# DeltaNet values turned by VectorE and a transfer instead of by TensorE

## The chip, the cores and the metric

The kernel runs on one core of a Trainium2 chip. The metric is the device time of one execution in microseconds (us), taken as the median of several runs. A profile is one further execution, recorded by the hardware; its span goes from the first to the last instruction.

## What is computed

One layer of a hybrid decoder on x of 1024 tokens by 2048 channels in float32, and a final RMSNorm. An input projection of the normalised x gives the columns of three groups: a gated MLP with mixing along the sequence (4 groups of 128), a gated DeltaNet (8 heads of 128), and cross-attention into 256 memory tokens (4 heads of 128). An output projection adds their gated outputs to x. What matters here is the DeltaNet and its values v:

```python
qkv = causal_conv_silu(jnp.concatenate([d_q, d_k, d_v], axis=-1), conv_w[l])
q, k, v = jnp.split(qkv, 3, axis=-1)
...
g = -jnp.exp(dn_a_log[l]) * jax.nn.softplus(d_a + dn_dt_bias[l])
beta = jax.nn.sigmoid(d_b)
o = gated_delta_rule(q, k, v, g, beta)   # per head, chunk by chunk along the tokens
o = rmsnorm(o, dn_norm_g[l]) * jax.nn.silu(d_z)
```

The causal convolution runs along the tokens, four taps per channel. Inside the delta rule each token's row of v is multiplied by a scalar of that token.

## The kernel before

The tokens are handled in two halves (`hf`) of 512, each of which is four tiles of 128 tokens (`NT = 4`). The projections are the bulk of TensorE's work: `project_stage` and `seven` run seven products over blocks of weights in place of eight (sums and differences of operand blocks are formed first), and each float32 operand is split into a high and a low part (`rhi`, `rlo`, `lh`, `ll`), three matmuls per product. They accumulate in the PSUM tiles `acc` and, in some stages, `dn2` and `dn3`. The weights come as tiles `raw` and `kept`, the left operands as `ll` and `lm`.

The DeltaNet runs beside the projections. A head's queries, keys and values are written by the projection to memory (`p_d`) with the channels on the partitions and the tokens along the row, since that suits the convolution. `front` prepares the queries and keys of a pair of heads for one half; `inverse` and `levels` invert the triangular matrices of the chunks; `back_of` calls `front_late` (loads what `front` stored), `levels`, `values`, and `back`, which makes the four `scan_step`s over token tiles and then `heads_out`. There are four pairs of heads and two halves, so `back_of` runs eight times: pairs 0 and 1 for both halves, each followed by a `front` of pair 2 or 3, and later pairs 2 and 3 for both halves.

`values` runs `conv` (one scaling on ScalarE, three multiply-adds on VectorE, SiLU on ScalarE) into a tile `v` of the ring `tn`. The scan wants the tokens on the partitions. So `to_tokens` has TensorE transpose the four 128x128 tiles of `v` against the identity into a PSUM bank (`scan_banks`), and `by_token` scales them, one ScalarE instruction per tile, into the head's `vs`.

The outputs of the heads take another way back to channels on partitions. `turn` has VectorE transpose a 128x512 tile in blocks of 32x32 and stores it to memory, `turned_in` loads it in four transfers, each of which puts one row of blocks in its place, and `normed` reads the loaded tile in the view `four(..., "b t i")`, which walks over four runs of 32 elements. The same pair of helpers is used for the gate (`gate`) and for the gated MLP (`gated`, `spatial`).

The ring `tn` has four tiles, handed out in turn. `values` takes one per head, `qk` (in `front`) one per head for a broadcast row, `all_sums` three per call, and the ring `sums` of the attention stage contains them too. One of the four is taken out of the ring for good ahead of the last four `back_of`:

```python
el = over([abh[:, 0:HT], ring["tn"].bufs.pop()])
```

No instruction goes straight to an engine. Every call is recorded in a `Plan` with its dependencies, and `Plan.issue` lays them all out: `lay` simulates the five engines and the DMA engines with costs per instruction, `late` computes due times from the end, and of nine such layouts the one that the simulation gives the earliest end is issued. Each engine then works through its list in order. All loads and stores named here are issued by SyncE's queue (`Q`). Line 398 of the profile is the line on which all recorded instructions are issued, so groups are told apart by the names of their tiles.

Of the kernel before, what the change touches and what calls it, by code (L numbers as in the profile page):

```python
# [11 lines left out]
AF = mybir.ActivationFunctionType  # L12
# [5 lines left out]
P = 128  # L18
# [4 lines left out]
HT = 512  # L23
# [3 lines left out]
NG, NH, NX = 4, 8, 4  # L27
# [374 lines left out]
def kernel(  # L402
# [29 lines left out]
    V, S, G, PE, Q = R.dve, R.act, R.pool, R.pe, R.sp  # L432
    rank, behind = R.rank, R.behind

    def C(shape, name, dt=F32):
        return sb.tile(list(shape), dt, name=name, tag=name)[:]

    def DT(shape, name, dt=F32):
        return dr.tile(list(shape), dt, name=name, tag=name)[:]
# [41 lines left out]
    def tok(ap):  # L481

        return ap.rearrange("p (t c) -> p t c", c=P)
# [15 lines left out]
    ring = {t: Slots(t, 2, [P, HT]) for t in ("kT", "qT", "vs", "kd", "ai")}  # L499
# [6 lines left out]
    jk = C([P, HT], "jk", mybir.dt.bfloat16)  # L506
# [4 lines left out]
    turn = {"acc": 0, "tp": 0, "dn": 0}  # L511
# [224 lines left out]
    for mt in range(2):  # L736
        t = [ring["ai"](F32R) for _ in range(2)]
# [9 lines left out]
    for h in range(NX):  # L747
        t = ring["vs"](F32R).rearrange("p (s m) -> p s m", s=2)
# [60 lines left out]
    def over(bufs):  # L809
        r = Ring("", 0, None)  # L810
        r.bufs = bufs
        return r
# [38 lines left out]
    r3, ww = ([steps[:, i * P : (i + 1) * P] for i in two] for two in ((0, 1), (2, 3)))  # L851
    scs = [C([P, 12, NT, NH], f"sc{hf}") for hf in range(2)]
    gcs, ecs = ([DT([NT, NH, P], f"{n}{hf}") for hf in range(2)] for n in ("gcd", "ecd"))
    e_d = [[DT([P, NT, P], f"ed{hf}_{h}") for h in range(NH)] for hf in range(2)]
    scan_banks, work = dnr.bufs[0:2], over(dnr.bufs[0:2])
    dnab = over(scan_banks)
# [68 lines left out]
    def to_tokens(*pairs):  # L925
        with R.together():
            for src, tp in pairs:
                for tt in range(NT):
                    PE.transpose(tp[:, tt * P : (tt + 1) * P], src[:, tt * P : (tt + 1) * P], ident)
        return [tok(tp) for src, tp in pairs]  # L930

    def four(t, order):

        return t.rearrange(f"p ({order}) -> p t b i", b=4, t=NT)

    def turn(tile, src, dst):

        V.transpose(four(tile, "b t i"), four(src, "t b i"))
        Q.dma_start(dst, tile)

    def turned_in(o, src):

        v = src.rearrange("(a j) (b n) -> b j a n", a=4, b=4)
        for b in range(4):
            Q.dma_start(o[b * 32 : (b + 1) * 32].rearrange("j (a n) -> j a n", a=4), v[b])

    def conv(which, h, hf, o):
        ct = which * NH + h
        xr = ring["xr"]()
        w = [cw[:, k * 24 + ct : k * 24 + ct + 1] for k in range(4)]  # L950
        if hf == 0:
            G.memset(xr[:, 0:3], 0.0)
            Q.dma_start(xr[:, 3:], p_d[which][h][:, 0:HT])
        else:
            Q.dma_start(xr, p_d[which][h][:, HT - 3 :])
        S.activation(o, xr[:, 3:], AF.Copy, scale=w[3])
        for k in range(3):
            V.scalar_tensor_tensor(o, xr[:, k : k + HT], w[k], o, op0=ALU.mult, op1=ALU.add)
        S.activation(o, o, AF.Silu)

    def by_token(o, src, scale):
        for tt in range(NT):
            S.activation(o[:, tt], src[:, tt], AF.Copy, scale=scale[:, tt : tt + 1])

    def sumsq(o, src):
        for tt in range(NT):
            S.activation(jk[:, 0:P], src[:, tt], AF.Square, accum_out=o[:, tt : tt + 1])

    def qk(h, hf, tiles, hs, gt, bank):

# [2 lines left out]
        beta, edk = (scs[hf][:, i] for i in (0, 4))  # L973
        (kt,) = to_tokens((k, bank))
        sumsq(hs[:, 1], kt)
        V.tensor_scalar(hs[:, 1], hs[:, 1], EPS, None, op0=ALU.add)
        V.reciprocal(hs[:, 3], hs[:, 1])
        V.scalar_tensor_tensor(hs[:, 2], hs[:, 3], -1.0, beta[:, :, h], op0=ALU.mult, op1=ALU.mult)
        V.tensor_tensor(out=hs[:, 3], in0=hs[:, 2], in1=edk[:, :, h], op=ALU.mult)
        by_token(kd, kt, hs[:, 3])  # L980
        e = tok(ring["E"]())
        Q.dma_start(e, e_d[hf][h])
        Q.dma_start(vs, ecs[hf][:, h].partition_broadcast(P))
        by_token(e, e, hs[:, 2])
        (qt,) = to_tokens((q, bank))
        sumsq(hs[:, 0], qt)
        V.tensor_scalar(hs[:, 0], hs[:, 0], P * EPS, P * EPS * EPS, op0=ALU.mult, op1=ALU.add)
        rsqrt_to(hs[:, 4], hs[:, 1])
# [170 lines left out]
    def heads_out(hf, hp, hss, rest):  # L1159
        obs = [vs for kd, ai, vs in rest]  # L1160

        for hs, ob in zip(hss, obs):
            sumsq(hs[:, 5], ob)
            V.scalar_tensor_tensor(hs[:, 6], hs[:, 5], 1.0 / P, hs[:, 0], op0=ALU.mult, op1=ALU.add)
            rsqrt_to(hs[:, 7], hs[:, 6])
            by_token(ob, ob, hs[:, 7])
        for h, (kd, ai, vs) in zip(hp, rest):
            kd, ai, y = (t.rearrange("p t c -> p (t c)") for t in (kd, ai, vs))
            turn(kd, y, o_d[hf][h])
            if h >= NJ:  # L1170
                e = sums()
                Q.dma_start(e, g_d[hf][h - NJ])
                turned_in(ai, o_d[hf][h])
                normed(kd, ai)
                V.tensor_tensor(out=y, in0=kd, in1=e, op=ALU.mult)
                head_done(h, hf, y)
# [36 lines left out]

    def values(hf, hp, gt, qs, ks, hss, rest, inv):
        for i, h in enumerate(hp):
            v = ring["tn"]()
            conv(2, h, hf, v)
            bank = scan_banks[i]
            by_token(rest[i][2], to_tokens((v, bank))[0], hss[i][:, 4])

    def back(hf, hp, gt, qs, ks, hss, rest, inv, ut=None):
        ut = ut or levels(gt, *inv)
# [339 lines left out]
    scan_banks, work = [dnr.bufs[0]] * 2, over(dnr.bufs[0:1])  # L1562
    gdrs = []

    def back_of(p, hf, inv):
        state = front_late(p, hf, inv)
        ut = levels(state[2], *state[-1])
        values(*state)
        back(*state, ut)
# [106 lines left out]
    scan_banks, work = dnr.bufs[0:2], over(dnr.bufs[2:3])  # L1676
# [46 lines left out]
    for n, (tag, to) in enumerate((("gt", mkT), ("inv", mv))):  # L1723
        for i in range(NX // 2):
            t = ring[tag](F32R).rearrange("p (h s m) -> p h s m", h=2, s=2)
# [107 lines left out]
    tn = ring["tn"].bufs  # L1833
# [88 lines left out]
```

## Time and profile before

| | |
|---|---|
| median of 3 runs | 1594.69 us (1593.5 to 1596.71) |
| profiled execution: its own time | 1593.81 us |
| profiled execution: span | 1592.1 us |
| mean granted TensorE clock | 0.997 |
| busy: TensorE, its weight loads | 1570.2 us, 1315.3 us |
| busy: VectorE, ScalarE, GpSimd | 1228.7 us, 963.3 us, 106.7 us |
| moved by the DMA engines | 434.12 MB, 273 GB/s on average |

The busy time of TensorE contains the modelled ends of pipelined matmuls: a 128x512 matmul lasts 0.39 us in the records, but the next one starts 0.23 us after it. The span is shorter than the profiled execution's own time by what lies around the first and last instruction. A row of a group of instructions has the engine, the operation, what it writes and reads, its count, the busy time and the mean time of one in ns, and then the idle time of its engine ahead of it with what ended that. A row of a tile has count, shortest, median and longest duration in ns, and the starts of the first and last in us. A row of a stretch has its length and for each engine the busy time and the number of instructions, then the granted clock, the busy share of the DMA engines and GB/s. A row of the timeline has the start and the length in us.

### The profile page before, as it was taken

Reading aid. Unit: us, or ns where it says so; the run is one execution under the profiler, and the core shown is the slowest. Engines: PE = TensorE matmul, PEld = TensorE weight load, DVE = VectorE, ACT = ScalarE, POOL = GpSimd, SP = SyncE. Lnnn points to the kernel's source line nnn. Section 1 sums busy time; section 2 is a strip of 40 time slices with the busy share of each in tenths; the row PEclk is TensorE's granted clock in tenths of the full one; section 3 lists DMA queues with packets and bytes.
Section 4 is the critical chain, followed back from the end, with each engine's and each line's share of the span. In section 5 each row is a group of like instructions: output and inputs, shape, how many; then the busy total and the mean of one; then the engine's idle time right before and its main releaser. Section 6 shows DMA issues by size and latency. Waiting matters only on the chain.

```text
span 1592.1 us, 24568 instructions
## 1 busy us (share of the span) xinstructions
PE 1570.2 (99%) x8349; PEld 1315.3 (83%) x8349; DVE 1228.7 (77%) x1818; ACT 963.3 (61%) x2006; POOL 106.7 (7%) x143
## 2 busy tenths in 40 slices
PE   8999999999999999999999989999999999999997
PEld 7988888888887888888888878888888888888886
DVE  6977655877589997777789996867658888688875
ACT  6833255535698436787886557765658864344455
POOL 0100010001000100111111001000000000000001
PEclk9999999999999999999999999999999999999999
DMA  9999966888679898786888988999877989778647
GB/s 320 327 317 346 284 171 183 294 292 245 218 246 315 298 325 254 257 250 205 282 281 277 303 244 245 341 325 309 268 245 253 298 298 347 235 263 293 232 146 276
DMA packets 335951, 434.12 MB, mean 273 GB/s; under 512 B 70089, under 2 KB 160466, under 8 KB 335826
## 3 DMA queue, kind: packets, MB, share of 16 engines
q1 hardware_dynamic: 334098, 429.39, 83.3%
q0 software_dynamic: 1088, 2.10, 0.4%
q8 instruction: 66, 1.08, 0.3%
q10 hardware_dynamic: 640, 1.07, 0.2%
q14 instruction: 59, 0.48, 0.1%
HBM read 332.78 MB, written 99.16 MB: 271 GB/s over the span
## 4 chain that ended last, share of the span: by engine, by line
PE 92%; ACT 3%; DMA 2%; DVE 1%; issue 1%; SPq 0%; POOL 0%; POOLq 0%; ACTq 0%; DVEq 0%
PE acc L398 56%; PE dn L398 35%; ACT jk L398 1%; ACT rhi L398 1%; DMA h0d<-tn 1%; SPq L398 0%; DMA tn<-vd 0%; DMA ut<-in_x_dram 0%; DMA kept<-in_mem_dram 0%; DVE rlo L398 0%; DMA raw<-in_w_in_dram 0%; DVE vs L398 0%; ACT vs L398 0%; DVE tn L398 0%; ACT inv L398 0%
## 5 line engine op out<-in xcount | busy, mean ns | idle before, releaser
L398 PE MATMUL acc<-lh,rhi 128*128 128x512 f32 x1024 | 396.2, 396 | 2.9 <-DVE obs L398 1.2
L398 PE MATMUL acc<-lh,rlo 128*128 128x512 f32 x1024 | 382.9, 397 | 0.0
L398 ACT CAST rhi<-raw 128x1024 fp32r<-128x1024 f32 (+1 forms) x148 | 186.6, 1261 | 248.8 <-PE dn L398 133.8
L398 DVE TENSOR_TENSOR rlo<-raw,rhi 128x1024 fp32r<-128x1024 f32 (+1 forms) x148 | 219.3, 1482 | 109.0 <-ACT rhi L398 98.8
L398 PE MATMUL acc<-ll,rhi 128*128 128x512 f32 x688 | 268.0, 395 | 0.8 <-DVE ll L398 0.8
L398 PEld LDWEIGHTS acc<-lh,rhi 128*128 128x128 f32 x1024 | 192.3, 188 | 41.1 <-issue 1.5
L398 PEld LDWEIGHTS acc<-lh,rlo 128*128 128x128 f32 x1024 | 191.9, 188 | 37.4
L398 DVE TENSOR_TENSOR ll<-ll,lh 128x1024 fp32r<-128x1024 f32 x122 | 148.5, 1217 | 17.3 <-ACT lh L398 17.0
L398 PEld LDWEIGHTS acc<-ll,rhi 128*128 128x128 f32 x688 | 129.6, 189 | 26.4 <-DVE ll L398 1.3
L398 ACT CAST lh<-ll 128x1024 fp32r<-128x1024 f32 x122 | 128.2, 1051 | 29.5 <-PE dn L398 9.0
L398 PE MATMUL acc<-lm,rhi 128*128 128x512 f32 x336 | 130.6, 394 | 0.0
L398 PE MATMUL dn<-lh,rhi 128*128 128x512 f32 x288 | 112.6, 393 | 0.0
L398 PE MATMUL dn<-lh,rlo 128*128 128x512 f32 x288 | 109.7, 393 | 0.0
L398 DVE TENSOR_TENSOR raw<-raw,kept 128x1024 f32<-128x1024 f32 (+1 forms) x56 | 80.9, 1444 | 6.9 <-DMA raw<-in_w_in_dram 5.9
L398 DVE TENSOR_TENSOR rlo<-kept,rhi 128x1024 fp32r<-128x1024 f32 (+1 forms) x29 | 41.8, 1443 | 47.3 <-ACT rhi L398 44.4
L398 PE MATMUL dn<-ll,rhi 128*128 128x512 f32 x192 | 75.2, 393 | 0.0
L398 PEld LDWEIGHTS acc<-lm,rhi 128*128 128x128 f32 x336 | 63.2, 188 | 11.9
L398 ACT CAST rhi<-kept 128x1024 fp32r<-128x1024 f32 (+1 forms) x29 | 35.6, 1229 | 50.3 <-PE dn L398 26.2
L398 PEld LDWEIGHTS dn<-lh,rhi 128*128 128x128 f32 x288 | 54.1, 188 | 10.6
L398 PEld LDWEIGHTS dn<-lh,rlo 128*128 128x128 f32 x288 | 54.0, 188 | 10.5
L398 POOL TENSOR_TENSOR hs<-hs,mhalf 128x4 f32<-128x4 f32 x32 | 48.4, 1515 | 195.3 <-DVE hs L398 194.9
L398 POOL TENSOR_TENSOR small<-small,mhalf 128x1 f32<-128x1 f32 x26 | 21.6, 832 | 562.8 <-DVE small L398 562.8
(421 smaller groups left out, 3449.6 us busy)
## 6 DMA issues: line engine op xcount, KB each, us to landing
raw<-in_w_in_dram SPq DMA_DIRECT2D x120, 512.0 KB
ll<-hsd SPq DMA_DIRECT2D x54, 512.0 KB
raw<-in_w_out_dram SPq DMA_DIRECT2D x48, 512.0 KB
raw<-in_w_in_dram SPq DMA_DIRECT2D x72, 256.0 KB
lm<-hsd SPq DMA_DIRECT2D x26, 512.0 KB
pd<-obs SPq DMA_DIRECT2D x48, 256.0 KB
late<-os SPq DMA_DIRECT2D x44, 256.0 KB
kept<-in_w_in_dram SPq DMA_DIRECT2D x20, 512.0 KB
```

The lines of the kernel that those rows point to most:

```text
L398: o.fn(*o.args, **o.kw)
```

## The change

The values go the way of the heads' outputs. `values` takes a second tile of `tn` per head. VectorE transposes `v` into it in 32x32 blocks and it is stored to a new buffer in memory, `vt_d` (`turn`); four transfers bring it back into `v` with the rows of blocks exchanged (`turned_in`). `by_token` reads it from SBUF in the view `four(v, "b t i")`, and the new helper `like` gives its output the same shape. The four TensorE transposes of each head and half are gone, and with them the use of a PSUM bank there.

```diff
@@ -851,6 +851,7 @@
+    vt_d = [[DT([P, HT], f"vtd{hf}_{h}") for h in range(NH)] for hf in range(2)]
@@ -960,11 +961,15 @@
     def by_token(o, src, scale):
         for tt in range(NT):
-            S.activation(o[:, tt], src[:, tt], AF.Copy, scale=scale[:, tt : tt + 1])
+            S.activation(like(o[:, tt], src), src[:, tt], AF.Copy, scale=scale[:, tt : tt + 1])
 
     def sumsq(o, src):
         for tt in range(NT):
-            S.activation(jk[:, 0:P], src[:, tt], AF.Square, accum_out=o[:, tt : tt + 1])
+            S.activation(like(jk[:, 0:P], src), src[:, tt], AF.Square, accum_out=o[:, tt : tt + 1])
+
+    def like(o, src):
+
+        return o.rearrange("p (b i) -> p b i", b=4) if len(src.shape) == 4 else o
@@ -1213,10 +1218,11 @@
     def values(hf, hp, gt, qs, ks, hss, rest, inv):
         for i, h in enumerate(hp):
-            v = ring["tn"]()
+            v, t = ring["tn"](), ring["tn"]()
             conv(2, h, hf, v)
-            bank = scan_banks[i]
-            by_token(rest[i][2], to_tokens((v, bank))[0], hss[i][:, 4])
+            turn(t, v, vt_d[hf][h])
+            turned_in(v, vt_d[hf][h])
+            by_token(rest[i][2], four(v, "b t i"), hss[i][:, 4])
```

## The prediction

> **What bounds the kernel now.** I read the page first: busy shares and the chain that ended last; then TensorE's timeline where the step lies; then stretches of the span, for what is short there besides TensorE.
>
> ```profile
> PE 1570.2 (99%) x8349; PEld 1315.3 (83%) x8349; DVE 1228.7 (77%) x1818; ACT 963.3 (61%) x2006; POOL 106.7 (7%) x143
> ...
> PE 92%; ACT 3%; DMA 2%; DVE 1%; issue 1%; SPq 0%; POOL 0%; POOLq 0%; ACTq 0%; DVEq 0%
> ```
>
> ```profile
> core 0: us, PE busy (x) PEld busy (x) DVE busy (x) ACT busy (x) POOL busy (x), PEclk, DMA share, GB/s
> 130.00:1340.00 1210.00, 1203.24 (x6521) 1004.36 (x6519) 939.29 (x1417) 766.83 (x1688) 90.37 (x113) 1.00 0.85 273
> 910.00:935.00 25.00, 20.90 (x84) 16.10 (x83) 23.74 (x51) 11.08 (x15) 1.24 (x2) 0.93 0.97 296
> 985.00:1110.00 125.00, 124.16 (x800) 105.01 (x799) 94.47 (x128) 83.25 (x176) 7.46 (x12) 1.00 0.99 330
> 1110.00:1262.00 152.00, 152.00 (x868) 128.71 (x867) 115.28 (x179) 105.14 (x245) 7.30 (x7) 1.00 0.80 259
> ```
>
> TensorE is busy for 99% of the span and makes 92% of the chain that ended last. Between 130 and 1340 us it stands still for 1210.00 - 1203.24 = 6.8 us in all. So a TensorE instruction taken out there shortens the kernel by its slot, as long as what replaces it delivers in time. The replacement uses VectorE (77% busy), SyncE's queue and the DMA engines (83%). Two stretches are tight: from 910 to 935 us VectorE is busy for 23.74 of 25 us, and there TensorE loses 4.1 us; from 985 to 1110 us the DMA engines are 99% busy.
>
> **TensorE: the removed transposes.** The values of a head and half, 128 channels by 512 tokens, are turned by four transposes.
>
> ```profile
> L398 PE MATMUL dn<-ident,tn x64: 270/272/328, 617.1 to 1168.4; 128*128 128x128 f32 x64
> L398 SPq DMA_DIRECT2D sd<-tn x22: 319/362/916, 1176.6 to 1338.0; - x22
> ```
>
> ```profile
> 620.10 0.39 PE L398 MATMUL acc<-ll,rhi 128*128 128x512 f32 x1
> 620.33 0.60 PE L398 MATMUL dn<-ident,tn 128*128 128x128 f32 x4
> 620.68 0.48 PE L398 MATMUL acc<-lh,rlo 128*128 128x512 f32 x1
> 621.00 0.39 PE L398 MATMUL acc<-lh,rhi 128*128 128x512 f32 x1
> 621.23 0.40 PE L398 MATMUL acc<-ll,rhi 128*128 128x512 f32 x1
> ```
>
> The 64 transposes lie between 617 and 1168 us, inside the full stretch, and at the median of 272 ns they are alike. Their 272 ns overlap: what counts is how far they push the next matmuls. Matmuls of the stream start 0.23 us apart. From the group's start at 620.33 to the second matmul behind it at 621.00 are 0.67 us (the first one behind starts 0.35 later, and the next only after 0.32); without the group one interval of 0.23 would stand there. So a group costs 0.67 - 0.23 = 0.44 us, and 16 groups 16 x 0.44 = 7.0 us. The transposes do not lie in idle time, so they cannot come out for nothing. **-7.0 us.** The Trainium skill, "TensorE: Matmul & The Clock Gate", Part 4, puts a 128x128 transpose at about 275 ns in one kernel's context. The row agrees as to the duration, 272 ns; charged to TensorE's time, as an estimate from that page, 64 of them would be 17.6 us.
>
> **VectorE and ScalarE.** The nearest rows are those of the outputs of the same heads, which already go this way.
>
> ```profile
> L398 ACT ACTIVATE vs<-vs,hs 128x128 f32<-128x128 f32 x64 | 21.0, 395 | 0.7 <-POOL hs L398 0.7
> ...
> L398 ACT ACTIVATE vs<-dn,hs 128x128 f32<-128x128 f32 x64 | 18.6, 376 | 5.3 <-PE dn L398 5.1
> ...
> L398 ACT ACTIVATE os<-xr,cw 128x512 f32<-128x512 f32 x22 | 16.0, 728 | 10.2 <-DMA late<-os 5.9 <-DMA xr<-pd 2.4 <-DVE inv L398 1.4
> ...
> L398 DVE STREAM_TRANSPOSE kd<-vs 128x512 f32<-128x512 f32 x16 | 11.3, 704 | 4.5 <-ACT vs L398 4.5
> ...
> L398 ACT ACTIVATE kd<-ai,col 128x512 f32<-128x512 f32 x8 | 5.7, 721 | 0.0
> ```
>
> Sixteen VectorE transposes of exactly this shape stand in the trace at 704 ns, so 16 more are 11.3 us on an engine with some 360 us free. They cost nothing where TensorE's matmuls hide them, which is everywhere but from 910 to 935 us, where VectorE is full and TensorE waits behind it. Bounds: none of the new ones lands there (0) or the four of two head pairs do (4 x 0.70 = 2.8 us). I take one, since a stretch of 25 us is small against 550: **+0.7 us.**
>
> ScalarE's 64 scalings read SBUF instead of PSUM: 395 against 376 ns, 64 x 0.019 = 1.2 us on an engine 61% busy. Reading in four blocks of 32 costs nothing: 721 ns in that view (`kd<-ai,col`) against 728 ns in a plain one. **0**, hidden by TensorE; without that cover 1.2 us.
>
> **SyncE and the DMA engines.** Each head and half gets one store of 256 KB and four loads of 64 KB, 80 issues in all. The output path shows them.
>
> ```profile
> L398 SPq DMA_DIRECT2D ai<-od x32: 302/430/700, 1010.2 to 1221.2; - x32
> L398 SPq DMA_DIRECT2D od<-kd x16: 319/335/430, 653.7 to 1216.0; - x16
> ```
>
> ```profile
> 1131.83 0.32 SPq L398 DMA_DIRECT2D od<-kd  x1
> ...
> 1137.48 1.87 SPq L398 DMA_DIRECT2D ai<-od  x4
> 1139.45 0.40 SPq L398 DMA_DIRECT2D raw<-in_w_in_dram  x1
> ...
> 1142.70 1.74 SPq L398 DMA_DIRECT2D ai<-od  x4
> ```
>
> ```profile
> SPq L398 <- DMA od<-kd: 4.0, 4, 2.1
> ```
>
> The issues of one head take 0.34 + 4 x 0.43 = 2.1 us of SyncE's queue, 33 us in all. Behind them stand the loads of weight blocks (`raw`) and of left operands, which TensorE needs some chunks later. The load that waits for the store's landing could hold those up. In the output path that wait was 4.0 us over 4 cases of 16, at worst 2.1 us, because the planner puts other issues between store and load, as the rows show. And in 1110 to 1262 us, with two such bursts in these rows, TensorE is busy for all of 152.00 us. So **0** in the forecast; the bounds are 0 and 16 x 2.1 = 33 us if no burst were hidden, the first by far the nearer to the row.
>
> For the DMA engines there are two readings of the queue's row on the page (packets, MB, share of 16 engines).
>
> ```profile
> q1 hardware_dynamic: 334098, 429.39, 83.3%
> ```
>
> By bytes: 83.3% of 1592.1 us for 429.39 MB is 3.1 us per MB, and 0.52 MB per head are 1.6 us. By packets: the same 1326 us over 334098 packets are 4.0 ns each, and 128 + 512 rows give 2.5 us. So 26 to 40 us over the kernel, beside 15% of free DMA time between 130 and 1340 us (180 us). **0** in the sum; what it costs where nothing is free is a rival below.
>
> **The sum.** -7.0 + 0.7 = -6.3 us. The profiled execution took 1593.81 us (span 1592.1 and 1.7 around it), 0.9 us under the median of 1594.69. So 1587.5 for it and **1588.4** for the median. This case's own range: down to 1583, if the new order of work (the planner lays out all instructions anew) also loses some 5 of the 6.8 us that TensorE waits now; up to 1591, with the VectorE bound of 2.8 us in full.
>
> **Rivals.**
>
> *The DMA engines take it back.* From 985 to 1110 us they have 1% of 125 us, 1.3 us, free. At an even pace over the 551 us of the transposes, 125 us hold about two of the eight head pairs. Four heads need 4 x 1.6 to 4 x 2.5 = 6.5 to 10 us. If TensorE waits for what does not fit, 5 to 9 us come back: by the first, 1588.4 + 5.2 = 1593.6, no change. For it: the 0.99. Against it: TensorE works 124.16 of those 125 us, and the stretch behind has 20% free, into which work that is not urgent can move.
>
> *Slower: a round trip through memory takes the place of the transposes, in the `tn` tiles.* Now a pair's eight scalings come in one go:
>
> ```profile
> 1168.09 1.66 ACT L398 ACTIVATE vs<-dn,hs 128x128 f32<-128x128 f32 x6 [0.32 <-PE dn L398]
> ```
>
> In the output path a tile needs this long from VectorE's transpose to ScalarE's use:
>
> ```profile
> 1131.09 0.71 DVE L398 STREAM_TRANSPOSE kd<-vs 128x512 f32<-128x512 f32 x1 [1.41 <-ACT vs L398]
> ```
>
> ```profile
> 1144.48 0.73 ACT L398 ACTIVATE kd<-ai,col 128x512 f32<-128x512 f32 x1
> ```
>
> That is 1144.48 - 1131.09 = 13.4 us. It is hidden where the convolved values lie ready early. But after the change each head takes two `tn` tiles. For the first four pairs there are four, which `front` uses too; for the last four there are three, so the second head's turned tile is the one in which the first head's values wait for their scaling, and that waits until the pair before has given `vs` free. The second head's round trip then starts only there, 13.4 us per pair. The sums behind use the same three tiles (`all_sums`, `mix_done`), and they end just in time:
>
> ```profile
> L398 SPq DMA_DIRECT2D lm<-sd x11: 360/367/378, 1332.9 to 1561.4; - x11
> ```
>
> ```profile
> L398 SPq DMA_DIRECT2D mixd<-vs x8: 320/384/580, 1022.8 to 1233.4; - x8
> ```
>
> The output projection first reads sums at 1332.9, and the last ones from `tn` are stored at 1338.0. If the last pair's 13.4 us pass through to them, TensorE waits as long: 1588.4 + 13.4 = 1601.8. It decides from 6.3 us of delay passed on. Against it: the last DeltaNet output is stored at 1233.4, 99 us before the first sum is read, and all but the last pairs' delay should drown in that. The Trainium skill, "VectorE: DVE Perf Modes", Rules for kernel authors, takes this side: a 128x128 transpose belongs on TensorE where a PSUM result is acceptable, and VectorE's is for single 32x32 blocks. By latency the rows agree (0.67 us against 13.4); by time on the engine that bounds, they don't.
>
> *The slots are worth more than their spacing.* If each transpose cost TensorE its whole 272 ns, 64 x 0.272 = 17.4 us would go: 1593.81 - 17.4 + 0.7 + 0.9 = 1578.0. The timeline's 0.44 us per group speaks against it: the matmul behind the four starts 0.35 us after the first of them. The page named above for the 275 ns would, read so, be on this side.
>
> **Chances.** Forecast 0.53; whole durations 0.02; DMA engines 0.17; the round trip 0.28, since the planner's model of a transfer has to hold for 16 new ones and nearly every wait that it misses lands on a full TensorE. 0.2%, 3.2 us, is about what can be told from no change: faster 0.55, the same 0.17, slower 0.28. The range goes from 1583 to 1606 (1601.8 and some 4 us for the same bounds); it leaves out perhaps 0.05 below and 0.14 above.
>
> **What would show it.** Right: no `dn<-ident,tn`; 32 VectorE transposes of 0.70 us in the DeltaNet part; TensorE still above 1195 of 1203 us between 130 us and the output projection, which starts some 6 us earlier. DMA rival: stretches at 0.99 that have grown longer, with TensorE waiting for `rhi` or `lh` there. Round trip: ScalarE's scalings of a pair's second head 10 us or more behind the first's, and TensorE idle near the first `lm<-sd`. The forecast is wrong if TensorE's idle time within the span grows by more than 3 us.

## The result and the profile after

| | before | after |
|---|---|---|
| median | 1594.10 us (1593.49 to 1596.71, 4 runs) | 1619.20 us (1617.76 to 1619.57, 4 runs) |
| profiled span | 1592.1 us | 1617.4 us |
| mean granted TensorE clock | 0.997 | 0.992 |
| TensorE idle within the span | 21.9 us | 41.1 us |

After stands to before as 1.0153, with an interval of [1.0135, 1.017]. The change makes the kernel 25 us slower. The forecast was 6 us faster, and 1619.2 lies outside its range.

These are the rows of the page of the kernel after: busy times, the DMA queue, and the chain that ended last.

```profile
PE 1576.3 (97%) x8285; PEld 1313.6 (81%) x8285; DVE 1241.4 (77%) x1834; ACT 971.6 (60%) x2008; POOL 99.0 (6%) x143
...
q1 hardware_dynamic: 345618, 437.78, 84.5%
...
PE 83%; DMA 6%; ACT 4%; DVE 3%; SPq 1%; issue 1%; POOL 0%; POOLq 0%; ACTq 0%; DVEq 0%
```

TensorE has 64 instructions fewer and is busy for longer. Of the 25.3 us that the span has grown, 19.2 are idle time of TensorE and 6.1 are busy time. The busy time hides a gain: a clock of 0.992 over 1617.4 us loses 12.9 us, 0.997 over 1592.1 us loses 4.8, so, as an estimate from these means, up to 8 us are work at the lower clock. TensorE's share of the chain fell from 92 to 83%, and DMA, ScalarE and VectorE have taken it over.

Where the time went shows in the stretches. First two of before that the prediction did not show, then after (columns as in the prediction: length, busy time of each engine, granted clock, DMA share, GB/s).

```profile
615.00:830.00 215.00, 214.84 (x1411) 182.85 (x1410) 169.61 (x290) 173.69 (x510) 28.38 (x30) 1.00 0.80 253
830.00:985.00 155.00, 150.89 (x786) 124.17 (x785) 137.40 (x237) 93.54 (x162) 13.84 (x18) 0.99 0.86 263
```

```profile
130.00:1340.00 1210.00, 1184.43 (x6352) 982.59 (x6351) 934.04 (x1413) 763.28 (x1672) 82.63 (x113) 0.99 0.86 274
615.00:830.00 215.00, 208.35 (x1386) 173.27 (x1384) 160.51 (x258) 159.21 (x439) 17.07 (x26) 0.99 0.83 259
830.00:985.00 155.00, 140.94 (x714) 113.53 (x713) 133.08 (x242) 90.62 (x188) 16.39 (x19) 0.96 0.85 262
985.00:1110.00 125.00, 123.62 (x802) 103.45 (x801) 92.47 (x137) 90.02 (x195) 10.04 (x15) 1.00 0.98 305
1110.00:1340.00 230.00, 227.77 (x1235) 192.03 (x1234) 184.87 (x279) 160.88 (x348) 6.88 (x8) 0.99 0.90 297
```

TensorE's idle time grows by 6.5 us from 615 to 830 us and by 10.0 us from 830 to 985 us (14.06 against 4.11), where the clock also falls to 0.96. From 985 to 1110 us, the stretch full of transfers that the prediction feared, it stands still for 1.4 us against 0.8. Setting the n-th projection matmul of one trace against the n-th of the other dates the loss: the one that before starts at 798 us starts 5 us earlier after the change, the one of 853 us 7 us later, that of 900 us 22 us later, that of 926 us 28 us later. From there to the end the delay stays between 20 and 28 us.

What TensorE waited for, its longest rows after:

```profile
PE acc L398 <- ACT lh L398: 5.3, 4, 2.2
PE dn L398 <- ACT os L398: 4.6, 1, 4.6
PE acc L398 <- DVE obs L398: 3.0, 1, 3.0
```

`os` is `front`'s tile, `lh` and `obs` are work of ScalarE and VectorE for the projections and the gated MLP. None is a row of the values. So the delay reaches TensorE through something between. The head pairs show where it begins. Below are, before and then after, the scan's ScalarE steps of the first four pairs (their last start is the end of the fourth pair's scan), and the loads with which the second call of `inverse` begins.

```profile
L398 ACT ACTIVATE steps<-dn x32: 254/273/303, 623.7 to 809.3; 128x128 f32<-128x128 f32 x32
```

```profile
L398 SPq DMA_DIRECT2D inv<-gdr x16: 275/293/304, 858.9 to 867.5; - x16
```

```profile
L398 ACT ACTIVATE steps<-dn x32: 258/272/279, 625.8 to 855.8; 128x128 f32<-128x128 f32 x32
```

```profile
L398 SPq DMA_DIRECT2D inv<-gdr x16: 262/294/348, 894.2 to 901.6; - x16
```

The first pair starts and ends where it did. The fourth ends 46 us later, and `inverse` follows 35 us late. Before, the last scan steps of the four pairs lie at 644.6, 696.6, 749.9 and 809.3 us; after, at 646.5, 715.7, 787.8 and 855.8. A pair takes about 70 us instead of 52 to 59. The timeline of after shows it (single rows of three engines in order of time; the many rows between them are left out):

```profile
660.08 0.40 ACT L398 ACTIVATE vs<-tn,hs 128x128 f32<-128x128 f32 x1
665.99 0.37 SPq L398 DMA_DIRECT2D tn<-ecd  x1
678.76 0.69 DVE L398 TENSOR_TENSOR os<-os,tn 128x512 f32<-128x512 f32 x1 [0.98 <-PE dn L398]
679.48 0.71 DVE L398 STREAM_TRANSPOSE tn<-tn 128x512 f32<-128x512 f32 x1
681.08 0.38 SPq L398 DMA_DIRECT2D vtd<-tn  x1
685.65 2.04 SPq L398 DMA_DIRECT2D tn<-vtd  x4
693.78 1.28 ACT L398 ACTIVATE vs<-tn,hs 128x128 f32<-128x128 f32 x4
726.85 0.69 DVE L398 TENSOR_TENSOR os<-os,tn 128x512 f32<-128x512 f32 x1 [1.28 <-PE dn L398]
748.46 0.69 DVE L398 TENSOR_TENSOR os<-os,tn 128x512 f32<-128x512 f32 x1 [3.90 <-PE dn L398]
749.73 0.70 DVE L398 STREAM_TRANSPOSE tn<-tn 128x512 f32<-128x512 f32 x1
817.65 0.68 DVE L398 TENSOR_TENSOR os<-os,tn 128x512 f32<-128x512 f32 x1
818.96 0.67 DVE L398 STREAM_TRANSPOSE tn<-tn 128x512 f32<-128x512 f32 x1
```

`os<-os,tn` is the product in `front` that reads its broadcast row, the last use of that `tn` tile. Three times the transpose of a pair's second head starts within 0.7 us of the end of such a product. The ring says why. Per pair, `values` now takes four tiles and `front` two, from a ring of four. The tile into which the second head is turned is the one that `front`'s second row had. So this chain stands in each period: `front`'s second product (678.8), transpose of the second head (679.5), store, loads, scaling of the second head (693.8), scan (last step 715.7). The round trip of 693.78 - 679.48 = 14.3 us stands in it with nothing beside it in the chain; the next two take 12.0 and 12.8 us. `front`'s products for the next pair come after that scan, at 726.9 and 748.5, and hold the next second head in their turn. TensorE transposes the first of these heads' keys at 690.7, but ScalarE takes them up only at 721.6, behind the scan in its list; why the planner put them there is not shown. By the ring, `front`'s next first row goes into the tile in which the first head's values wait for their scaling, and it is loaded at 666.0, just when that scaling has ended. But a row loaded then is read at 726.9 at the earliest, so this wait is not felt here.

Before the change a pair took four tiles, the ring came round once per pair, and both heads were scaled 4 us apart:

```profile
667.37 1.14 ACT L398 ACTIVATE vs<-dn,hs 128x128 f32<-128x128 f32 x4
...
671.26 1.13 ACT L398 ACTIVATE vs<-dn,hs 128x128 f32<-128x128 f32 x4
```

### The profile page after: what moved, and what is told of

Its sections match the earlier page's. It is cut to its first block, busy times and chain, and to the rows that moved or that the text cites. A ratio compares the mean times of both kernels' runs of the same rounds, so it can differ in the third digit from the quotient of the medians.

```text
span 1617.4 us, 24563 instructions
## 1 busy us (share of the span) xinstructions
PE 1576.3 (97%) x8285; PEld 1313.6 (81%) x8285; DVE 1241.4 (77%) x1834; ACT 971.6 (60%) x2008; POOL 99.0 (6%) x143
## 3 DMA queue, kind: packets, MB, share of 16 engines
q1 hardware_dynamic: 345618, 437.78, 84.5%
## 4 chain that ended last, share of the span: by engine, by line
PE 83%; DMA 6%; ACT 4%; DVE 3%; SPq 1%; issue 1%; POOL 0%; POOLq 0%; ACTq 0%; DVEq 0%
PE acc L398 50%; PE dn L398 34%; SPq L398 1%; DMA vd<-sm 1%; DMA raw<-in_w_in_dram 1%; DMA tn<-ecd 1%; ACT jk L398 1%; ACT vs L398 1%; DMA ll<-h0d 1%; ACT rhi L398 1%; DVE rlo L398 0%; POOL small L398 0%; DMA qT<-late 0%; DMA kept<-in_mem_dram 0%; ACT lh L398 0%
## 5 line engine op out<-in xcount | busy, mean ns | idle before, releaser
L398 DVE TENSOR_TENSOR lm<-lm,lh 128x1024 fp32r<-128x1024 f32 x42 | 51.2, 1220 | 9.5 <-ACT lh L398 9.2
```

What stands on the lines that cost most here:

```text
L398: o.fn(*o.args, **o.kw)
```

## The experiments

The theory, T: the second `tn` tile per head couples `values` and `front` in the ring, and the exposed round trip makes the first four pairs late; TensorE loses when late `front` and `inverse` meet the next stage. The rivals: the transfers and transposes themselves cost the time, or the last four pairs with their three tiles do (the prediction's rival), or the new order that the planner lays out. `h < NJ` are the heads 0 to 3, which the first four calls of `back_of` handle. A ratio is that to before, run on the same chip. Times of before there: 1594.66 us (e1, e2, e3, e5), 1595.49 (e4, e6, e7, e8), 1594.11 (e9, e10), 1593.99 (e11, e12).

**e1: the change without the second `tn` tile.** The turned tile goes into the `xr` tile that the convolution has just read.

```diff
         S.activation(o, o, AF.Silu)
+        return xr
...
-            v, t = ring["tn"](), ring["tn"]()
-            conv(2, h, hf, v)
-            turn(t, v, vt_d[hf][h])
+            v = ring["tn"]()
+            xr = conv(2, h, hf, v)
+            turn(xr[:, 0:HT], v, vt_d[hf][h])
```

> The change with one thing different: the turned tile is put into the `xr` tile that the convolution has just read, so each head takes one `tn` tile again, as before. All transfers and VectorE transposes of the change stay. Theory T (the second `tn` tile per head ties `values` to `front`, so that a pair's second head starts its round trip only when `front` is done with the tile): 1584 to 1592 us, the 7 us of TensorE slots come out. Rival R1 (the 80 issues and 8.4 MB of transfers delay the weight loads): about as the change, 1610 to 1620. Rival R2 (any new order of the planner loses against that of before): 1598 to 1620.

Measured: 1589.77 us, ratio 0.9969 [0.9959, 0.9979]. All 80 transfers and 16 transposes are there, and it is faster than both kernels. Its fourth pair ends at 799.3 us, and in its stretches TensorE has back most of what after lost, from 830 to 985 us all of it:

```profile
130.00:1340.00 1210.00, 1200.15 (x6473) 1001.11 (x6472) 952.13 (x1438) 774.23 (x1693) 84.43 (x113) 1.00 0.87 281
615.00:830.00 215.00, 211.45 (x1377) 179.68 (x1376) 169.01 (x291) 171.92 (x507) 18.66 (x28) 0.99 0.86 274
830.00:985.00 155.00, 153.35 (x807) 126.68 (x806) 137.59 (x240) 93.37 (x163) 13.69 (x17) 1.00 0.85 256
```

So the whole loss hangs on the second `tn` tile of a head.

**e2: before, with an unused `tn` tile per head.** The ring turns as fast as after the change, with no round trip.

```diff
+            ring["tn"]()
             v = ring["tn"]()
```

> The kernel before, in which `values` takes a second `tn` tile per head and does nothing with it; the values still go through TensorE, and no transfer is added. T: a second head's convolution has to wait for `front`, some 8 to 10 us per pair (convolution 5 us, transposes, scaling) where the change has 15 us, so half of the loss or more: 1603 to 1615 us. R1: no transfers, no loss: 1593 to 1596. R2: a new order too, 1598 to 1620, without a longer period from pair to pair.

Measured: 1597.34 us, ratio 1.0015 [1.0003, 1.0026]. The ties alone delay the fourth pair's scan by 25 us, to 833.8 us, and `inverse` by 11, to 870 us, and cost hardly 3 us. T had put half of the loss or more here, 1603 to 1615 us, and was wrong in that. The ties alone cost little; the loss comes when the round trip stands in the chain as well.

**e3: what the slots are worth.** Against before:

```diff
-            bank = scan_banks[i]
-            by_token(rest[i][2], to_tokens((v, bank))[0], hss[i][:, 4])
+            by_token(rest[i][2], tok(v), hss[i][:, 4])
```

> The kernel before without any transpose of the values (the scaling reads the untransposed tile; this part of the computation is left out). It shows what the 64 transposes are worth. T and R1: 7.0 us less than before, 1585 to 1589 us. R2: no gain, 1594 to 1615.

Measured: 1589.01 us, ratio 0.9967 [0.9955, 0.9978], that is 5.3 us below before. The interval is 3.5 to 7.2 us, so the prediction's 7.0 us is within it, and whole durations, 17.4 us, are excluded. e1 does all of the new work and is 0.8 us slower, less than the intervals tell apart: the work itself is nearly free.

**e4 and e5: half of the change.** e4 has TensorE transpose in the first four pairs and leaves the change in the last four; e5 is the other way round.

```diff
-            v, t = ring["tn"](), ring["tn"]()
+            v = ring["tn"]()
             conv(2, h, hf, v)
+            if h < NJ:    # e4; e5: h >= NJ
+                by_token(rest[i][2], to_tokens((v, scan_banks[i]))[0], hss[i][:, 4])
+                continue
+            t = ring["tn"]()
```

(In e5 the condition and the tile `t` come ahead of the convolution.)

> The counterpart of the run with the first four pairs: the first four go through TensorE as before, the last four by VectorE and memory in `tn` tiles as in the change. If the two halves of the change add up, 1594.7 + (1619.2 - 1611.8) = 1602 us. T with slack (the pairs may slip some 20 us before TensorE waits): the first four keep their pace and the last four have slack to the output projection, so 1589 to 1597 us, 3.5 us of slots gained. R1 (transfers): 1590 to 1596 as well, since the run with the turned tile in `xr` left nothing for it.

> The change for the first four head pairs only, those that run beside `front` on four `tn` tiles; the last four pairs go through TensorE as before. T as seen in the trace of the change, where the period from pair to pair in the first four grows from 50 to 70 us: nearly the whole loss, 1610 to 1618 us. The mechanism that the prediction named (three tiles in the last four pairs): little loss, 1591 to 1598. R1: half of the transfers, half of the loss, about 1604 to 1608.

Measured: e4 1597.54 us, 1.0014 [1.0002, 1.0026]; e5 1611.82 us, 1.0108 [1.0093, 1.0123]. Most of the loss comes from the first four pairs, where the prediction had seen no cost; e5 lies in T's range, its fourth pair ends at 848.1 us and its `inverse` starts at 889, 5 us ahead of after. The last four, where it had placed the round trip, cost a little; e4 lies 0.5 us above T's range. Together the two halves make 0.0108 + 0.0014 = 0.0122 of the 0.0153, so together they cost some 5 us more than one by one.

**e6 and e7: `front`'s row out of the ring, into `xr`.** e6 is the change with this edit, e7 is e1 with it.

```diff
-        kd, ai, vs = map(tok, (*tiles[2:4], ring["tn"]()))
+        kd, ai, vs = map(tok, (*tiles[2:4], xr[:, 0:HT]))
```

> The change with two `tn` tiles per head as it is, but `front` keeps its broadcast row in the `xr` tile of its own convolution instead of in `tn`. So the tie between `values` and `front` is cut on the other side. T: the fourth pair's scan ends near 800 us again instead of 856, and the time is 1586 to 1596 us. If instead the number of tiles per head or the transfers were to blame: 1610 to 1619 us.

> Both cuts at once: turned tile in `xr` and `front`'s row in `xr`, so `tn` holds nothing but the convolved values. T: no tie is left, but none was felt in the run with the turned tile in `xr` either (scan of the fourth pair at 799 us), so the same as that run within the planner's scatter: 1586 to 1592 us. If ties still cost something there: 1580 to 1585.

Measured: e6 1614.95 us, 1.0127 [1.0099, 1.0154]; e7 1600.50 us, 1.0028 [1.0012, 1.0044]. Both miss what T had said. e7 shows why e6 is no fair trial: holding `front`'s row in the `xr` tile costs 0.0028 + 0.0031 = 0.0059, 9.4 us, on a kernel without any tie in `tn`. A tie in `xr` seems to have taken the place of the one in `tn`: in both the fourth pair's scan ends at 833 to 834 us. With that and the 0.0060 of the last four pairs (below) on top of e1's 0.9969, e6 would be at 1.0088; the other 0.004 are unexplained. In e2 too that scan ends at 833.8 us. With the same delay of the pairs e2 costs 3 us, e7 5 and e6 19 against before, so the end of the fourth pair alone does not set the time; how late pairs turn into idle time of TensorE is only in part shown here.

**e8: only the first head keeps two tiles,** so that a pair takes five.

```diff
-            v, t = ring["tn"](), ring["tn"]()
-            conv(2, h, hf, v)
-            turn(t, v, vt_d[hf][h])
+            v = ring["tn"]()
+            t = None if i else ring["tn"]()
+            xr = conv(2, h, hf, v)
+            turn(xr[:, 0:HT] if i else t, v, vt_d[hf][h])
```

> A smaller dose: the first head of a pair takes two `tn` tiles, the second one only one and has its turned tile in `xr`. Five tiles per pair and `front` instead of six. The second head's values then wait for `front`'s first head, which ends some 20 us before its second. T: the fourth pair's scan ends between 800 and 830 us, and with 20 us of slack the time is 1587 to 1597 us. If any second tile per head costs in proportion: about 1605.

Measured: 1593.86 us, 0.9987 [0.9972, 1.0002]. This is within T's range of 1587 to 1597. Without the second head's turned tile in the ring no loss against before is left.

**e9 and e10: the same cut with a tile that is free.** Between the two calls of `inverse`, which work in it, the tile `abh[:, 0:HT]` lies unused. e9 puts `front`'s row for pairs 2 and 3 there and leaves two `tn` tiles to each head; e10 puts the turned tile there in the first four pairs.

```diff
-        kd, ai, vs = map(tok, (*tiles[2:4], ring["tn"]()))
+        kd, ai, vs = map(tok, (*tiles[2:4], abh[:, 0:HT] if h >= NJ else ring["tn"]()))   # e9
...
-            v, t = ring["tn"](), ring["tn"]()
+            v = ring["tn"]()
+            t = abh[:, 0:HT] if h < NJ else ring["tn"]()   # e10
```

> The change, but the broadcast row of `front` for pairs 2 and 3 lies in the free tile `abh[:, 0:HT]` instead of a `tn` tile; the values keep their two `tn` tiles per head. This cuts the tie between `values` and `front` without putting a new one on `xr`, as the run with the row in `xr` did (there the tie on `xr` by itself showed some 10 us, by the run with both in `xr`). Theory T (values and front wait on each other in the shared ring, six takes per pair for four tiles): the fourth pair's last scan step ends by about 800 to 820 us instead of 855.8, the pairs come some 50 to 57 us apart instead of 70, and the time is 1590 to 1600. Rival (two tiles per head in a ring of four are enough for the loss, front or not: the second head's turned tile waits for the first head's scalings): the pairs stay at 65 to 70 us, and the time is 1608 to 1619.

> The change, but for the first four pairs the turned tile lies in the free tile `abh[:, 0:HT]` instead of a second `tn` tile; the last four pairs keep two `tn` tiles per head. All transfers and VectorE transposes stay. Theory T: one `tn` tile per head as before the change, so the fourth pair's last scan step ends by 800 to 820 us; what remains is the last four pairs' own cost, some 5 to 8 us over the run with the turned tile in `xr` everywhere: 1592 to 1600. Rival (the store and the four loads per head beside the first four pairs cost the time by themselves): 1608 to 1619.

Measured: e9 1602.36 us, 1.0046 [1.0031, 1.006]; e10 1601.75 us, 1.0050 [1.0034, 1.0066]. The scans end where T puts them, at 810.7 and 812.0 us:

```profile
L398 ACT ACTIVATE steps<-dn x32: 252/273/320, 627.8 to 812.0; 128x128 f32<-128x128 f32 x32
```

(That is e10, the view of the tile `steps` as above.) `inverse` starts at 858 us in both, as before the change. The times lie some 2 us above T's ranges and 6 us below the rivals'. e9 differs from after in nothing but the place of `front`'s row: the tie between `values` and `front` is worth 1.0153 - 1.0046 = 0.0107, 17 us of the 25.

**e11 and e12: what is left.** Both have no second tile in the first four pairs (`abh` in e11, `xr` in e12). e11 has none in the last four either; e12 has `tn` there.

```diff
+            t = abh[:, 0:HT] if h < NJ else xr[:, 0:HT]       # e11
+            t = xr[:, 0:HT] if h < NJ else ring["tn"]()       # e12
```

> The change with no second `tn` tile at all: the turned tile lies in `abh[:, 0:HT]` in the first four pairs and in the `xr` tile that the convolution has just read in the last four. It differs from the run with `abh` in the first four pairs (1601.75 against 1594.11 us) in the last four alone. If what was left there is the last four pairs' second `tn` tile (the fifth pair's second head's turned tile waits for its first head's scalings, which are 29 us apart in that run, and VectorE is full near 930 us): scalings of the fifth pair's two heads within 10 us, TensorE idle in 830 to 985 us 4 us or less instead of 8.5, and 1588 to 1594. Rival (the rest is the transfers' and the `abh` tile's own cost in the first four pairs): still 1599 to 1604.

> The change with the turned tile in `xr` in the first four pairs and a second `tn` tile in the last four. By the reading that the last four pairs' second `tn` tile costs some 8 us (TensorE transposes in the first four and `tn` in the last four were 1597.5, and two TensorE-free halves with `xr` were 1589.8): 1594 to 1600, scalings of the fifth pair's heads over 20 us apart. Rival (the last four cost little, and the rest was the first four's): 1588 to 1592.

Measured: e11 1592.83 us, 0.9990 [0.9981, 1.0]; e12 1598.43 us, 1.0029 [1.0018, 1.0041]. Ratios to before, by where the turned tile lies:

| first four pairs | last four: `xr` | last four: `tn` |
|---|---|---|
| `xr` | 0.9969 (e1) | 1.0029 (e12) |
| `abh` | 0.9990 (e11) | 1.0050 (e10) |
| `tn` | not run | 1.0153 (after) |
| TensorE transposes | 1 (before: TensorE in all) | 1.0014 (e4) |

The columns of the first two rows differ by 0.0060 both times: the second `tn` tile costs 9.6 us in the last four pairs. (Each variant is laid out anew by the planner. How much of a difference of a few us comes from the new order alone, as in the 0.0021 between the two rows, no run tells.) Most of it falls from 830 to 985 us, at the fifth pair. There TensorE is busy for this long in e10, e11 and e12:

```profile
830.00:985.00 155.00, 146.54 (x789) 119.20 (x788) 133.82 (x238) 91.24 (x164) 12.86 (x19) 0.98 0.85 256
```

```profile
830.00:985.00 155.00, 150.12 (x780) 123.83 (x779) 138.36 (x242) 96.03 (x167) 15.51 (x17) 0.98 0.87 262
```

```profile
830.00:985.00 155.00, 146.21 (x805) 119.66 (x804) 136.24 (x245) 94.78 (x173) 14.33 (x19) 1.00 0.88 264
```

With `tn` TensorE stands still for 8.5 and 8.8 us there; with `xr` for 4.9 in e11 and 1.65 in e1. That is 7.1 us between e12 and e1, but only 3.6 between e10 and e11; e10 stands still for another 3 us longer behind 985 us. Through which wait, stays open. The idle time is spread over waits of 3 us and less, for operands of the projection that ScalarE and VectorE make. The distance of the fifth pair's scalings does not tell it: 29 us in e10 and 24 in e12, but also 17 in e11, where less than 10 was expected (and 4 us of idle time or less). In e1 and e11 both transposes of that pair are over by 873 us; in e4, e10 and e12 the second one comes at 896 to 914 us, where VectorE is nearly full. That fits, and was not tried by itself.

## Why the prediction was wrong

- **TensorE's slots.** -7.0 was forecast; e3 gives -5.3, and the interval takes in both. The method, spacing instead of durations, holds; the rival of whole durations falls. The new order that the planner lays out is in the measured value too.
- **VectorE and ScalarE: +0.7 and 0.** The durations were right; 0.7 us is less than the runs can tell apart (e1 against e3: 0.8 us). After, the 16 new transposes and the 64 scalings cost what the output path had shown, 704 ns and 393 against the 395 ns taken:

```profile
L398 ACT ACTIVATE vs<-tn,hs 128x128 f32<-128x128 f32 x64 | 21.8, 393 | 8.5 <-DMA tn<-vtd 3.9 <-DMA vd<-sm 3.2 <-DVE hs L398 1.3
...
L398 DVE STREAM_TRANSPOSE tn<-tn 128x512 f32<-128x512 f32 x16 | 11.3, 704 | 1.5 <-ACT vs L398 1.3 <-ACT tn L398 0.2
```

- **SyncE and the DMA engines: 0.** Right as to the work. The queue moved 8.39 MB and 11520 packets more; 84.5% of 1617.4 less 83.3% of 1592.1 us are 40 us, the upper of the two readings. And e1, which moves the same, is faster than before. The rival of full DMA engines falls.
- **The failed step is the latency of the round trip, in the first four pairs.** The prediction asked what the store, the loads and the wait in SyncE's queue cost as work, and what hid them. It had the 13.4 us of latency and the right tiles, but only in the rival, and there it followed the last four pairs. For the first four it noted that there are four tiles, "which `front` uses too", and went on. Had it written out six takes per pair from four tiles, it would have found the second head's transpose waiting for `front`'s second row, and the round trip behind that wait, in each pair. What it measured at: 12.0 to 14.3 us per round trip, 46 us at the fourth pair's end, 17 us of the time (e9). The sign that the prediction set for being wrong, more than 3 us more of idle time of TensorE, shows with 19.2.
- **The slower rival** had the mechanism and neither the place nor the size. Its mark, scalings of the second head 10 us or more behind the first's, is there: 660.1 and 693.8 in the second pair, and 14 to 18 us in each of the last three pairs. Its other mark is not: TensorE's idle time does not lie near the first `lm<-sd`, which starts 25.0 us late, at 1357.9 instead of 1332.9, as late as all that follows 926 us. The last four pairs cost 9.6 us, not by passing delay on to the output projection, but 400 us earlier. By the table the loss is 19.8 us in the first four (after against e12), 9.6 in the last four (e12 against e1), less the 4.9 that e1 gains. The field of the table that would show whether the two simply add was not run.
- **The bound of 33 us** for bursts in SyncE's queue would have covered the result, but for another reason, and it was not kept in the range.
- **The page's rule** (the Trainium skill, "VectorE: DVE Perf Modes", Rules for kernel authors: 128x128 on TensorE where PSUM will do) gave the right sign for the change as made. It does not decide here: e1 keeps the VectorE path and is 0.31% faster than TensorE's. What decides is which tile the latency holds.

## What to carry to other kernels

Before a short step is replaced by a long round trip, write out the order in which each ring's tiles are taken, by everyone who takes from it, and see whose last use each new tile waits for: with six takes from four tiles another part of the kernel came into the chain here. Price a latency in the chain that it enters and not by the engine that does the work; engines with free time are no cover for it. If the second tile can be one whose content has just been used up (here `xr`), the ring need not grow at all, as long as nobody else waits for that tile: with `front`'s row in `xr` as well, e7 was 9.4 us slower than e1.

## What the runs showed of the hardware

A stop of TensorE costs more than itself. The timeline of after, at its longest stop:

```profile
880.50 0.39 PE L398 MATMUL acc<-lh,rlo 128*128 128x512 f32 x1
885.53 1.12 PE L398 MATMUL dn<-ident,os 128*128 128x128 f32 x4 [4.64 <-ACT os L398]
886.30 0.78 PE L398 MATMUL acc<-lh,rhi 128*128 128x512 f32 x1
886.87 0.63 PE L398 MATMUL acc<-ll,rhi 128*128 128x512 f32 x1
887.30 0.63 PE L398 MATMUL acc<-lh,rlo 128*128 128x512 f32 x1
...
890.29 0.63 PE L398 MATMUL acc<-lh,rhi 128*128 128x512 f32 x1
890.71 0.47 PE L398 MATMUL acc<-ll,rhi 128*128 128x512 f32 x1
891.02 0.39 PE L398 MATMUL acc<-lh,rlo 128*128 128x512 f32 x1
```

After 4.64 us of waiting the matmuls start 0.43 us apart for 5 us, then 0.23 again; that loses some 2.2 us. A stop of 3.01 us at 946.62 does the same (`acc<-lh,rhi`, waiting for `obs`, the third row of waits above): the matmuls behind it start 0.43 us apart until 952 us, which loses 2.8 us. The Trainium skill, "TensorE: Matmul & The Clock Gate", Part 1, has half the clock after an idle window of some 3.4 us, and 426.7 ns from matmul to matmul at 512 columns then; the spacing agrees, and the stop of 3.01 us shows that a little less than the window can be enough. So these two stops cost, with the slow matmuls behind them, 1.5 and 1.9 times their own length, which the prediction's prices for waits left out. It is no fixed rule: in e1 TensorE stood still for 1.97 of the 3.5 us from 661.8 us on, and the granted clock was 0.50 from 665.3 to 668.7; in e2 a stop of 2.48 us that ended at 934.67 left it at 1.00 from 932 to 938. The rows of e1:

```profile
661.80:665.30 3.50, 1.53 (x8) 1.14 (x8) 3.17 (x10) 3.33 (x14) 0.11 (x1) 1.00 0.97 324
665.30:668.70 3.40, 3.40 (x12) 2.85 (x12) 3.40 (x5) 3.03 (x11) 0.00 (x0) 0.50 0.65 204
```
